# A two-layer hybrid decoder trunk on one core: the scheduler's timeline model in place of its default model

## The chip, the cores and the metric

The kernel runs on one core of one Trainium2 chip. The metric is the device time of one execution in microseconds. Three runs of the kernel before took 1592.68, 1589.84 and 1588.68 us; the median is 1589.84 us. Another execution was taken by the profiler: 1590.24 us, of which 1588.1 us lie between its first and last instruction (the span).

The engines are called as the profile calls them: PE (TensorE, matrix multiplication), PEld (its weight load), DVE (VectorE), ACT (ScalarE), POOL (GpSimd) and SP (SyncE, which issues all of this kernel's DMAs). Each engine works through a queue of its own in the order in which the program lists its instructions, and waits on semaphores for what other engines make.

## The reference

A trunk of two layers on 256 tokens of width 1024, all in float32. Each layer is a half-step SwiGLU network (inner width 2816), a token mixer, and a second half-step SwiGLU network; a last norm ends the trunk.

```python
for l in range(DEPTH):
    h = h + 0.5 * swiglu(rms_norm(h, ffn1_norm[l]), ffn1_w_in[l], ffn1_w_out[l])
    u = rms_norm(h, mix_norm[l])
    (z_s, xbc, dt_s, qkv, z_d, b_d, a_d, gate_s, gate_d) = jnp.split(u @ w_in[l], split_points, axis=-1)
    y_s = mamba2_branch(z_s, xbc, dt_s, ...)
    y_d = deltanet_branch(qkv, z_d, b_d, a_d, ...)
    merged = (jax.nn.sigmoid(gate_s) * (y_s @ ssm_w_branch[l])
              + jax.nn.sigmoid(gate_d) * (y_d @ dn_w_branch[l]))
    h = h + merged @ w_out[l]
    h = h + 0.5 * swiglu(rms_norm(h, ffn2_norm[l]), ffn2_w_in[l], ffn2_w_out[l])
return rms_norm(h, final_norm)
```

The Mamba-2 branch works on 32 heads in two chunks of 128 tokens: a short causal convolution, a decay matrix exp(a_i - a_j) for each head, and small products with it. The DeltaNet branch works on 8 heads in four chunks of 64 tokens: for each chunk a triangular matrix is inverted, and a state of 128 x 128 for each head goes from chunk to chunk.

## The kernel before

**The stream of weights.** All large weights lie in one array, cut into 504 halves of 128 x 1024 (512 KB). `load` (L95) issues the DMA of a half on SP into one of five `wraw` buffers. `prep` (L100) splits it for the products in fp32r: ACT rounds it into `whi` (L104), DVE subtracts to get the rest `wlo` (L105); there are five buffers of each. `take` (L113) hands the next half to the matmuls and traces the loads nine halves and the splits five halves ahead. A product is three matmuls: high by high, low by high and high by low (`mm3`, L210; `mm3w`, L215). The activations are split in the same way (`uTh`, `uTl`).

**The chunks.** `chan_chunk` (L238) takes two halves and runs 48 matmuls of 256 columns into one PSUM tile; `tok_chunk` (L221) and `out_chunks` (L257) run matmuls of 512 columns. Accumulators come from a pool of four PSUM tiles (`accp`), everything else that PE writes from another pool of four (`trp`). A pool `s2` of nine buffers holds the small intermediate tiles.

**The stages.** An FFN (`ffn`, L292) is 20 chunks of gate and up channels with a Silu on ACT and a product on DVE behind each, and then 22 rows of the output matrix. `close` (L275) ends each sub-layer: it adds to the residual `h` and starts the next norm (`norm_in`, L193) with raised priority, and `hold` keeps the splits of the next halves back until the norm's chain of ACT, DVE and POOL has been traced. `tc.issue_after(ins)` adds an edge that keeps instructions behind `ins` in the queue of its engine (L125, L205, L207, L334, L460, L605).

The mixer (`mixer`, L333) follows a hand-written list, `ORDER` (L38). Each word is a step: letters like `k`, `q`, `v`, `x`, `b`, `d`, `z`, `g` are chunks of weights with a convolution or an activation behind them; `K`, `Q`, `V` are the small products of a head pair; `I` the steps of the triangular inverse (`invert`, L596), `R` those of the recurrence (`recur`, L679), `D` a decay tile (`decay`, L793: a DMA of 1 MB into `dc`, two passes on DVE, an Exp on ACT, another pass on DVE), `S` and `T` the Mamba-2 products (`ssd`, L821), `N` the product with the DeltaNet output weights. The small products are in f32 and come in short bursts between the chunks.

**What sets the order.** The kernel doesn't list the queues itself. It traces its instructions, one after the other, into a tile context. When the context closes, a scheduler follows their dependencies and plays them through a model of the core's timing; whenever an engine of the model is free, it takes the ready instruction of the highest priority. The priority is the place in the trace, moved forward where `tc.high_priority` stands. The order in which the model took them becomes the order of each engine's queue, and the buffers of a pool are handed out in that order too. On the chip the queues run in that order, whatever the times really are. The context is opened in `kernel` (L1140):

```python
    with tile.TileContext(nc) as tc:
        trunk_kernel(tc, *args)
```

## Time and profile before

| | |
|---|---|
| median of three runs | 1589.84 us |
| profiled execution | 1590.24 us |
| its span | 1588.1 us |
| DVE, ACT and POOL busy | 1073.0, 879.0 and 55.1 us |
| mean granted clock of TensorE | 0.997 |
| DMA | 284.84 MB, 179 GB/s over the span |

The four FFNs take about 0 to 200, 600 to 800, 800 to 1000 and 1400 to 1588 us of the span, the two mixers about 200 to 600 and 1000 to 1400. In the answers of the trace, a row of a group gives the source line, the engine, the operation, the tiles as output<-inputs, the shapes and the count; behind the bar stand the busy time and the mean of one in ns, and behind the second bar the idle time just before them with what ended it. A row of a wait reads: engine, tile and line that waited, whom for, then the total in us, the number of times and the longest. The matmuls of PE overlap, so a row's duration is longer than the distance to the next start. The rows themselves stand in the prediction, where they are used.

### The profile page before, as it was taken

The numbers are of one execution on the slowest core, as the hardware profiler recorded it, in microseconds if no ns is written. First come the engines' busy times: TensorE is split into PE (matmuls) and PEld (weight loads), VectorE is DVE, ScalarE is ACT, GpSimd is POOL, SyncE is SP. The second block draws the span as 40 slices with busy tenths as digits, with TensorE's granted clock in tenths as the row PEclk, the third lists the DMA queues.
The fourth block names the chain that finished last, engine by engine and source line by source line (L and its number), as shares of the span: only waits on it lengthen the run. The fifth ranks groups of instructions, "written<-read, shape, count | busy, mean of one in ns | idle before, by whom it ended". The sixth has DMA issues, their size and how long they took to land.

```text
span 1588.1 us, 30449 instructions
## 1 busy us (share of the span) xinstructions
PE 1565.9 (99%) x12456; PEld 1459.8 (92%) x12456; DVE 1073.0 (68%) x1560; ACT 879.0 (55%) x1412; POOL 55.1 (3%) x60
## 2 busy tenths in 40 slices
PE   8999999999999999999999999999999999999998
PEld 7999879989999998999889987899899999989986
DVE  5555468966899766555465555698679996675554
ACT  5444468756566545444354444686655764454443
POOL 0000020000000000000000001100000000000000
PEclk9999999999999999999999999999999999999999
DMA  7555465552465446555565555655435555555552
GB/s 269 193 187 196 162 209 187 167 162 94 168 221 180 147 160 212 187 190 194 173 203 188 192 189 178 203 177 179 131 121 201 185 171 174 174 179 193 187 197 94
DMA packets 91922, 284.84 MB, mean 179 GB/s; under 512 B 22069, under 2 KB 23045, under 8 KB 90758
## 3 DMA queue, kind: packets, MB, share of 16 engines
q1 hardware_dynamic: 91782, 282.90, 53.7%
q8 instruction: 97, 1.59, 0.4%
q14 instruction: 43, 0.35, 0.1%
HBM read 280.94 MB, written 1.92 MB: 178 GB/s over the span
## 4 chain that ended last, share of the span: by engine, by line
PE 89%; DVE 5%; ACT 2%; DMA 2%; issue 1%; POOL 1%; SPq 0%; POOLq 0%; ACTq 0%; DVEq 0%
PE fc L218 9%; PE fc L217 9%; PE fc L219 9%; PE o L213 6%; PE o L211 6%; PE o L212 6%; PE b L219 3%; PE b L218 3%; PE b L217 3%; PE t L211 2%; PE t L212 2%; PE t L213 2%; PE xs L218 1%; PE xs L217 1%; PE xs L219 1%; DVE wlo L65 1%
## 5 line engine op out<-in xcount | busy, mean ns | idle before, releaser
L65 DVE TENSOR_TENSOR wlo<-wraw,whi 128x1024 fp32r<-128x1024 f32 x504 | 612.9, 1223 | 374.5 <-ACT whi L62 369.2
L62 ACT ACTIVATE whi<-wraw 128x1024 fp32r<-128x1024 f32 x504 | 529.5, 1059 | 433.7 <-PE fc L218 176.2
L217 PE MATMUL fc<-uTh,whi 128*128 128x256 f32 x1280 | 357.7, 279 | 0.0
L218 PE MATMUL fc<-uTl,whi 128*128 128x256 f32 x1280 | 357.3, 279 | 0.0
L219 PE MATMUL fc<-uTh,wlo 128*128 128x256 f32 x1280 | 357.3, 279 | 0.0
L218 PEld LDWEIGHTS fc<-uTl,whi 128*128 128x128 f32 x1280 | 240.6, 188 | 0.2
L217 PEld LDWEIGHTS fc<-uTh,whi 128*128 128x128 f32 x1280 | 240.6, 188 | 0.2
L219 PEld LDWEIGHTS fc<-uTh,wlo 128*128 128x128 f32 x1280 | 240.5, 188 | 0.0
L211 PE MATMUL o<-whi,gh 128*128 128x512 f32 x352 | 137.3, 390 | 0.0
L212 PE MATMUL o<-wlo,gh 128*128 128x512 f32 x352 | 137.2, 390 | 0.0
L213 PE MATMUL o<-whi,gl 128*128 128x512 f32 x352 | 137.0, 389 | 0.0
L217 PE MATMUL b<-bh,whi 128*128 128x256 f32 x384 | 107.8, 283 | 0.0
L218 PE MATMUL b<-bl,whi 128*128 128x256 f32 x384 | 106.8, 279 | 0.0
L219 PE MATMUL b<-bh,wlo 128*128 128x256 f32 x384 | 106.6, 279 | 0.0
L213 PEld LDWEIGHTS o<-whi,gl 128*128 128x128 f32 x352 | 66.1, 188 | 13.7
L212 PEld LDWEIGHTS o<-wlo,gh 128*128 128x128 f32 x352 | 66.1, 188 | 13.6
L211 PEld LDWEIGHTS o<-whi,gh 128*128 128x128 f32 x352 | 66.1, 188 | 13.4
L217 PE MATMUL xs<-uTh,whi 128*128 128x256 f32 x256 | 74.0, 289 | 0.0
L217 PE MATMUL g<-uTh,whi 128*128 128x256 f32 x256 | 73.0, 285 | 0.0
L218 PEld LDWEIGHTS b<-bl,whi 128*128 128x128 f32 x384 | 72.3, 188 | 0.0
L219 PEld LDWEIGHTS b<-bh,wlo 128*128 128x128 f32 x384 | 72.0, 188 | 0.0
L217 PEld LDWEIGHTS b<-bh,whi 128*128 128x128 f32 x384 | 71.8, 188 | 0.0
(264 smaller groups left out, 3224.5 us busy)
## 6 DMA issues: line engine op xcount, KB each, us to landing
wraw<-in_wst_dram SPq DMA_DIRECT2D x504, 512.0 KB, 4.2
dc<-rdram SPq DMA_DIRECT2D x8, 1024.0 KB, 8.0
nw<-in_norms_dram SPq DMA_DIRECT2D x6, 512.0 KB, 4.9
gb<-rdram SPq DMA_DIRECT2D x8, 256.0 KB, 5.6
h<-in_x_dram SPq DMA_DIRECT2D x4, 256.0 KB, 3.1
out_dram<-fo SPq DMA_DIRECT2D x4, 256.0 KB, 2.3
dq<-X SPq DMA_DIRECT2D x2, 256.0 KB, 4.5
cs<-in_cst_dram SPq DMA_DIRECT2D x1, 384.0 KB, 8.9
```

The costliest lines, as they stand in the source:

```text
L62: return A.activation(out=o, in_=i, func=func, **kw)
L65: return V.tensor_tensor(out=o, in0=a, in1=b, op=op)
L211: PE.matmul(ps, lh, rh, start=start, stop=False)
L212: PE.matmul(ps, lh, rl, start=False, stop=False)
L213: PE.matmul(ps, ll, rh, start=False, stop=stop)
L217: PE.matmul(ps, wh, mh, start=start, stop=False, skip_group_check=shared)
L218: PE.matmul(ps, wh, ml, start=False, stop=False, skip_group_check=shared)
L219: PE.matmul(ps, wl, mh, start=False, stop=stop, skip_group_check=shared)
```

## The change

The tile context is opened with one more argument. The scheduler then plays the traced instructions through another model of the core's timing, one built from lists of events (waits, engine and device holds, delays, semaphore updates), in place of the default model that gives each instruction a time on its engine. Nothing that `trunk_kernel` traces differs: the instructions, tiles, buffer counts, priorities and `issue_after` edges are the same.

```diff
-    with tile.TileContext(nc) as tc:
+    with tile.TileContext(nc, schedule_with_timeline_sim=True) as tc:
         trunk_kernel(tc, *args)
```

## The prediction

> **What bounds the kernel now.** The page comes first, for the whole span; then the table by stretches, because a mean hides stages with different limits; then what TensorE (PE) waited for.
>
> ```profile
> span 1588.1 us, 30449 instructions
> PE 1565.9 (99%) x12456; PEld 1459.8 (92%) x12456; DVE 1073.0 (68%) x1560; ACT 879.0 (55%) x1412; POOL 55.1 (3%) x60
> ```
> ```profile
> 100.00:200.00 100.00, 99.44 (x599) 88.51 (x598) 52.56 (x56) 44.83 (x53) 0.55 (x1) 1.00 0.54 181
> 300.00:400.00 100.00, 97.97 (x1020) 92.15 (x1019) 72.27 (x156) 61.58 (x145) 2.01 (x2) 0.98 0.46 143
> 400.00:500.00 100.00, 98.35 (x929) 95.99 (x928) 93.75 (x125) 65.88 (x91) 4.32 (x4) 1.00 0.56 187
> 1100.00:1200.00 100.00, 97.97 (x1082) 93.65 (x1081) 71.74 (x147) 61.42 (x135) 3.02 (x3) 1.00 0.44 141
> 1200.00:1300.00 100.00, 99.16 (x963) 96.57 (x962) 97.50 (x126) 65.86 (x89) 3.31 (x3) 1.00 0.56 193
> 1500.00:1588.00 88.00, 81.41 (x449) 70.74 (x447) 42.53 (x46) 34.27 (x44) 1.10 (x2) 0.97 0.45 150
> ```
>
> The columns after the stretch are its length, then busy microseconds of PE, weight load, DVE, ACT and POOL, then clock, DMA share and GB/s. PE is busy for 1565.9 of 1588.1 us: **22.2 us of idle PE** is the whole sum of visible gaps. 6.6 of it (88.00 - 81.41) is the end of the program, where the last norm and the stores have no matmul beside them. An FFN stretch (100 to 200) leaves 0.6 us. The mixers (about 200 to 600 and 1000 to 1400) leave 2.0 and 1.7 us in the two stretches of the first layer shown, 2.0 and 0.8 in those of the second. There DVE is nearly full as well: 93.75 and 97.50 of 100 us.
>
> ```profile
> PE hnT L186 <- DVE hn L68: 4.6, 7, 1.0
> PE xsb L835 <- ACT xsT L62: 2.5, 2, 1.6
> PE nw L157 <- DMA row<-in_norms_dram: 2.4, 1, 2.4
> PE bc L217 <- DVE ca L68: 2.0, 2, 1.0
> PE wb L627 <- ACT Y L62: 1.8, 2, 0.9
> PE f L211 <- ACT uTh L62: 0.7, 1, 0.7
> PE t L211 <- ACT uTh L62: 0.7, 1, 0.7
> ```
>
> These are all the waits of PE (total, times, longest): 14.7 us. Two kinds must be told apart. hnT, nw, f and t (8.4 us) stand at a norm or at the start, where the next matmul needs the whole residual or the first load: no other order finds work to put there, and `issue_after` and `hold` pin what surrounds them. xsb, bc and wb (6.3 us) stand inside the mixers, where PE sat at the head of its queue behind an instruction that came too early, while chunks of weights lay ready. Those 6.3 us are what a better order can take.
>
> **The change part by part.** It removes and adds no instruction of the kernel: the same matmuls, evictions and DMAs are traced, with the same tiles, buffer counts and explicit edges. What moves is the place of each in its engine's queue, and in SP's and POOL's. So the sum has three terms.
>
> *First, the early places that go.* If the other model puts the bursts of xsb, wb and the matmuls of bc where they are really ready, at best 6.3 us go; if it misjudges them as now, 0. The waits recur in both layers (twice each), so they come from a systematic misjudgement of a latency by the present order, which another model can cure or repeat. I take the middle, **-3 us**.
>
> *Second, the splits that come.* A burst of small f32 matmuls cut into a chunk costs something by itself:
>
> ```profile
> 479.93 0.28 PE L218 MATMUL b<-bl,whi 128*128 128x256 f32 x1
> 480.04 0.28 PE L219 MATMUL b<-bh,wlo 128*128 128x256 f32 x1
> 480.16 0.60 PE L890 MATMUL oT<-cs,vb 128*128 128x128 f32 x4
> 480.52 0.60 PE L217 MATMUL b<-bh,whi 128*128 128x256 f32 x3
> 480.95 0.28 PE L218 MATMUL b<-bl,whi 128*128 128x256 f32 x1
> ```
>
> Chunk matmuls start 0.11 to 0.12 us apart (479.93 to 480.04). After the burst, the three of L217, L218 and L219 that the row merges take 0.43 (480.52 to 480.95) where three steady ones take 0.35: 0.08 us, say **0.1 us a split**. From the code I count about 66 bursts in a layer (K, Q and V rests 20, scalars 5, masks 1, invert 8, recur 11, ssd 9, the turned operands of the two branches 12), 132 in all. If each were cut once more, as a model that fills every small gap might do, that is 13 us; none is 0; if it merged neighbours, up to some 3 us less. Both models fill gaps greedily, so I take a quarter more, **+3 us**.
>
> *Third, the queues of DVE, ACT and SP.* In the FFNs (about three fifths of the span) PE's own order can hardly change: one chunk follows another, each in a PSUM tile of its own, and the matmuls that accumulate into one tile depend on each other in order. What must not be late there is the split of the weights.
>
> ```profile
> L65 DVE TENSOR_TENSOR wlo<-wraw,whi 128x1024 fp32r<-128x1024 f32 x504 | 612.9, 1223 | 374.5 <-ACT whi L62 369.2
> L62 ACT ACTIVATE whi<-wraw 128x1024 fp32r<-128x1024 f32 x504 | 529.5, 1059 | 433.7 <-PE fc L218 176.2
> SPq L97 <- DVE wlo L65: 1129.0, 378, 17.4
> ```
>
> Each of the 504 halves costs 1.06 us on ACT and 1.22 on DVE. On average PE takes 1588.1 / 504 = 3.15 us for a half, so both keep up with room. ACT waits for PE to free a split buffer (176.2 us for fc alone), and SP waits 1129.0 us for DVE to free a raw buffer: the stream runs as far ahead as its five and five buffers let it. A shuffle of one or two microseconds there is hidden by these buffers: **0**. If that cover were gone, every late half would cost its lateness in full; the mixers' dense stretch is the only place where it nearly is, and that is the rival on the slow side. SP's other DMAs (8 of dc, 8 of gb, the gathers of the inverse) may change place among the loads of wraw; a block of SP that is no longer than the 17.4 us it already waits at its longest costs about nothing.
>
> The sum is -3 + 3 + 0 = 0. It is made against the profiled execution, 1590.24 us, that is the span of 1588.1 and 2.1 around it; this lies 0.4 above the median of the three runs, 1589.84. So I predict **1590 us**, with the bounds -6.3 - 3 (every avoidable wait gone, bursts merged) and +13 (every burst split) from the first two terms alone.
>
> **The rivals.**
>
> *A: faster, the better-timed order.* All three mixer waits go and a few bursts merge: 1590 - 6.3 - 2, about **1582**. For it: PE waits are the same ones in both layers. Against it: it needs nearly all of them, because anything under 4.8 us can't be told from no change, and the third term must stay at 0. More than this isn't there, since 8.4 us of waits and the end are dependencies.
>
> *B: slower, a DVE that is parked in its dense stretch.* Place: the decay tiles `dc`, at about 410 and 1200 us.
>
> ```profile
> 410.70 8.78 DMA dc<-rdram
> ```
> ```profile
> 416.76 1.23 DVE L65 TENSOR_TENSOR wlo<-wraw,whi 128x1024 fp32r<-128x1024 f32 x1 [0.17 <-ACT whi L62]
> 419.50 2.29 DVE L65 TENSOR_TENSOR dc<-dc,ac 128x2048 f32<-128x2048 f32 x1 [1.51 <-DMA dc<-rdram]
> ...
> 432.76 2.35 DVE L65 TENSOR_TENSOR wlo<-wraw,whi 128x1024 fp32r<-128x1024 f32 x2
> ```
> ```profile
> L65 DVE TENSOR_TENSOR dc<-dc,ac 128x2048 f32<-128x2048 f32 x4 | 9.1, 2285 | 1.5 <-DMA dc<-rdram 1.5
> ```
> ```profile
> 420.00:450.00 30.00, 30.00 (x295) 29.09 (x295) 29.03 (x35) 17.50 (x22) 1.92 (x1) 1.00 0.46 153
> 450.00:480.00 30.00, 28.35 (x283) 27.48 (x283) 30.00 (x47) 23.91 (x36) 1.39 (x2) 1.00 0.64 210
> ```
> ```profile
> 459.68 0.28 PE L219 MATMUL xs<-uTh,wlo 128*128 128x256 f32 x1
> 461.61 0.44 PE L835 MATMUL xsb<-cs,xsT 128*128 128x128 f32 x2 [1.65 <-ACT xsT L62]
> ```
>
> A load of dc takes 8.78 us to land; today DVE stands still only 1.5 us for it, because `wlo`, conv and recur instructions lie ahead of the subtraction in its queue. If the other model thinks the load shorter, or lets it start later, and puts the subtraction first, DVE stands still up to 8.78, that is 7.3 us more, with the wlo of the next halves behind it. From 420 to 480 it then works 59.03 of 60 us and can't make it up, and PE already runs short there (1.65 us at 461). So a parked load reaches PE almost in full: 7.3 us a layer, 14.6 in both, **about 1605**; with two of the four loads of a layer parked, 1619. It decides from the point where the extra stand exceeds DVE's spare in the stretch, 6.25 us in the first layer and 2.5 in the second (100 less 93.75 and 97.50), if none of the lead is left. For it: in this stretch two engines are full at once, so any other order is a risk and none a gain. Against it: a model that has the load shorter than it is would also have to find nothing ready to put before it.
>
> [...]
>
> *C: slower, more loads of the activation table.*
>
> ```profile
> L62 ACT ACT_TABLE_LOAD x30 | 38.5, 1283 | 16.6 <-DVE ca L68 15.4 <-PEq L1133 0.7
> ```
>
> The mixers mix Silu (conv, z), Exp (decay, masks) and Tanh (gates) on ACT; 30 loads stand there now. An order that interleaves them more finely adds 1.283 us of ACT for each. ACT has room (55% busy) except from 450 to 480, where 6.1 us are free: from the fifth added load in that stretch on (6.1 / 1.283 = 4.7), each costs PE 1.28 us. Doubling all 30 with a quarter of them uncovered gives 30 x 1.283 / 4, some 10 us: **1600**. [...]
>
> *D: the two models give the same order.* Then 1590, and the engines' sequences agree one by one. Possible for the FFNs, hardly for 800 us of mixers.
>
> **How the numbers follow.** A measurement of this kernel tells about 0.3% (4.8 us) from no change; its three runs before span 4.0 us. My forecast, little change from small gains and losses that offset, with D in it: 0.42, its own range 1585 to 1595. A: 0.20. B: 0.28. C and other misplaced bursts on PE: 0.10. So faster 0.20, the same 0.42, slower 0.38. The range goes down to 1581, just past A, because below it only the bound of 9.3 us is left, and up to 1612, between B with one load parked in each layer and B with two.
>
> **What would show it.** First term: the waits of PE for xsb, bc and wb shrink from 6.3 us. Second: more matmul groups of small shapes between chunk matmuls, with PE's busy time up by 0.1 us for each. Third: wlo and whi appear among PE's waits only if the cover is gone. B: in the waits of DVE, dc rises from 1.5 us in 420 to 520 and PE waits for wlo after it. C: the count of table loads over 30. The prediction is wrong if PE's idle time grows at the norms, where I hold the order to be pinned, if DMAs land late because SP was blocked over 17.4 us, or if the instruction counts change.

## The result and the profile after

The changed kernel is **slower by 4.2%**: 1658.54 us (median of four runs, 1654.84 to 1660.53) against 1590.67 us (four runs, 1588.68 to 1592.68); the ratio is 1.0424, 95% interval 1.0408 to 1.044. Its profiled execution took 1660.53 us with a span of 1658.7 us, 70.6 us longer than the span of before. The first two lines of its page:

```profile
span 1658.7 us, 30485 instructions
PE 1593.8 (96%) x12456; PEld 1481.0 (89%) x12456; DVE 1070.7 (65%) x1560; ACT 879.1 (53%) x1416; POOL 49.2 (3%) x60
```

The work is the same, and DVE and ACT are busy for as long as before (1070.7 and 879.1 us where it was 1073.0 and 879.0). PE is not: its idle time is 1658.7 - 1593.8 = 64.9 us instead of 22.2, which is 42.7 us more, and it is busy 27.9 us longer with the same 12456 matmuls. So there are two things to find: waits, and matmuls that last longer.

The table by stretches, with the cuts at the last `o` matmul of a sub-layer (columns as in the prediction); first two rows of the kernel before, the first mixer and the second FFN:

```profile
199.00:613.00 414.00, 409.04 (x3644) 384.32 (x3643) 326.86 (x550) 260.92 (x479) 22.85 (x22) 1.00 0.52 170
613.00:799.50 186.50, 185.83 (x1294) 172.37 (x1293) 103.70 (x114) 87.82 (x112) 2.02 (x2) 1.00 0.56 189
```

The same sub-layers of the changed kernel:

```profile
199.50:636.80 437.30, 418.95 (x3644) 392.63 (x3643) 326.99 (x550) 262.04 (x481) 21.26 (x22) 0.97 0.49 161
636.80:830.00 193.20, 188.18 (x1294) 174.12 (x1293) 103.06 (x114) 87.16 (x112) 1.11 (x2) 0.98 0.55 183
```

The mixer lost 23.3 us, the FFN 6.7. The second mixer and the two other FFNs behind a norm lost about as much each (23.8 and 7.5 to 9.0 us), and the first FFN, which has no norm between sub-layers ahead of it, 0.5. The column of the clock differs too: 0.97 and 0.98 where it was 1.00.

What PE waited for in the changed kernel (the largest rows of the view of waits):

```profile
PE f L213 <- DVE uTl L65: 13.0, 4, 4.2
PE t L213 <- DVE uTl L65: 8.4, 2, 4.2
PE b L217 <- DVE ca L68: 7.0, 2, 3.5
PE wb L627 <- ACT Y L62: 4.8, 4, 1.9
...
PE yb L627 <- DMA TT<-dq: 3.0, 2, 2.2
PE ydb L849 <- DVE xdt L65: 2.5, 2, 1.2
```

The first two rows, 21.4 us, did not exist before. They stand at the norms. DVE's timeline at the first norm between two sub-layers, in the kernel before (start, duration, what, count, and in brackets the idle time ahead of it and what ended it):

```profile
187.38 0.69 DVE L68 SCALAR_TENSOR_TENSOR h<-o,h 128x512 f32<-128x512 f32 x1 [1.08 <-PE o L213]
190.78 0.69 DVE L68 SCALAR_TENSOR_TENSOR h<-o,h 128x512 f32<-128x512 f32 x1 [2.71 <-PE o L213]
...
193.21 1.41 DVE L68 SCALAR_TENSOR_TENSOR hn<-h,zz,nw 128x512 f32<-128x512 f32 x2 [0.73 <-POOL zz L121]
194.54 1.22 DVE L65 TENSOR_TENSOR wlo<-wraw,whi 128x1024 fp32r<-128x1024 f32 x1
195.68 1.28 DVE L65 TENSOR_TENSOR uTl<-hnT,uTh 128x512 fp32r<-128x512 f32 x2
196.87 2.35 DVE L65 TENSOR_TENSOR wlo<-wraw,whi 128x1024 fp32r<-128x1024 f32 x2
```

The same place in the changed kernel:

```profile
193.44 1.29 DVE L68 SCALAR_TENSOR_TENSOR h<-o,h 128x512 f32<-128x512 f32 x2 [4.93 <-PE o L213]
...
197.43 1.42 DVE L68 SCALAR_TENSOR_TENSOR hn<-h,zz,nw 128x512 f32<-128x512 f32 x2 [0.73 <-POOL zz L121]
198.77 3.49 DVE L65 TENSOR_TENSOR wlo<-wraw,whi 128x1024 fp32r<-128x1024 f32 x3
202.17 0.68 DVE L68 SCALAR_TENSOR_TENSOR h<-o,h 128x512 f32<-128x512 f32 x1
202.78 1.21 DVE L65 TENSOR_TENSOR wlo<-wraw,whi 128x1024 fp32r<-128x1024 f32 x1
203.91 0.68 DVE L68 SCALAR_TENSOR_TENSOR h<-o,h 128x512 f32<-128x512 f32 x1
204.51 1.21 DVE L65 TENSOR_TENSOR wlo<-wraw,whi 128x1024 fp32r<-128x1024 f32 x1
205.64 1.28 DVE L65 TENSOR_TENSOR uTl<-hnT,uTh 128x512 fp32r<-128x512 f32 x2
```

Between `hn` and `uTl` stood one split of weights; now there stand five, and the residual of the other tokens. `uTl` starts 8.2 us after `hn` where it started 2.5 us after. `hn` is late as well: before, the two residual adds `h` started at 187.38 and 190.78, as PE finished one accumulator of `o` after the other; now both start at 193.44, because the order of the `o` matmuls among themselves has changed and both accumulators end late. What PE makes of it, in the kernel before:

```profile
194.02 0.66 PE L186 MATMUL hnT<-cs,hn 128*128 128x128 f32 x4 [0.56 <-DVE hn L68]
...
199.10 0.39 PE L211 MATMUL t<-whi,uTh 128*128 128x512 f32 x1
199.33 0.39 PE L212 MATMUL t<-wlo,uTh 128*128 128x512 f32 x1
```

And in the changed kernel:

```profile
199.59 1.03 PE L186 MATMUL hnT<-cs,hn 128*128 128x128 f32 x8
201.43 0.50 PE L211 MATMUL t<-whi,uTh 128*128 128x512 f32 x1 [0.81 <-ACT uTh L62]
...
206.38 0.79 PE L213 MATMUL t<-whi,uTl 128*128 128x512 f32 x1 [4.20 <-DVE uTl L65]
206.97 0.63 PE L211 MATMUL t<-whi,uTh 128*128 128x512 f32 x1
207.39 0.63 PE L212 MATMUL t<-wlo,uTh 128*128 128x512 f32 x1
```

Three things are to be seen. The transposes `hnT` stand behind all `o` matmuls (in the kernel before, at 194.02 in the midst of them, which last to 199.1), so nothing covers the chain from `hnT` over `uTh` to `uTl`: `hn` starts 2.2 us before the last `o` is through, where it started 5.9 us before. L213 stands 4.20 us for `uTl`. And the matmuls behind it start 0.42 to 0.43 us apart (206.97, 207.39, and so on to 210.38), where those of 128 x 512 start 0.23 apart otherwise (199.10 and 199.33 above): nine of them run slowed, some 1.7 us lost, with the granted clock at 0.50 from 204.2 to 211.0 us. Behind the start of the program I count ten such stretches in the trace by the distances between starts; the distances beyond the usual ones add up to 18.4 us, most of the 27.9 us that PE is busy longer. Between its start and its last norm the trace of before has one stretch of this kind, with a clock of 0.50 from 354.6 to 358.0 us; most of it falls on small products, and three matmuls of `bc` lose some 0.3 us. At the start of the program both kernels have it (the kernel before until 13.1 us, the changed one until 16.5).

### The profile page after: what moved, and what is told of

It reads as the page before. It is cut to its first block, busy times and chain, and to the rows that moved or that the text cites. A ratio compares the mean times of both kernels' runs of the same rounds, so it can differ in the third digit from the quotient of the medians.

```text
span 1658.7 us, 30485 instructions
## 1 busy us (share of the span) xinstructions
PE 1593.8 (96%) x12456; PEld 1481.0 (89%) x12456; DVE 1070.7 (65%) x1560; ACT 879.1 (53%) x1416; POOL 49.2 (3%) x60
## 4 chain that ended last, share of the span: by engine, by line
PE 76%; DVE 5%; DMA 2%; ACT 2%; issue 1%; SPq 0%; POOL 0%; POOLq 0%; DVEq 0%; ACTq 0%
PE fc L219 7%; PE fc L217 7%; PE fc L218 7%; PE o L213 4%; PE o L211 4%; PE o L212 4%; PE b L218 2%; PE b L219 2%; PE b L217 2%; PE xs L217 2%; PE xs L219 2%; PE g L217 2%; PE g L218 2%; PE xs L218 2%; PE g L219 2%; PE t L211 2%
## 5 line engine op out<-in xcount | busy, mean ns | idle before, releaser
L213 PE MATMUL o<-whi,gl 128*128 128x512 f32 x352 | 136.4, 389 | 0.0
L211 PE MATMUL o<-whi,gh 128*128 128x512 f32 x352 | 132.5, 389 | 0.0
L213 PEld LDWEIGHTS o<-whi,gl 128*128 128x128 f32 x352 | 66.1, 188 | 13.8
```

Source lines behind the costliest of these rows:

```text
L211: PE.matmul(ps, lh, rh, start=start, stop=False)
L213: PE.matmul(ps, ll, rh, start=False, stop=stop)
```

## The experiments

**How an order is put into a kernel.** Apart from `fence`, all kernels below use the default model, with the queue of every engine written out and forced by edges that make no engine wait for another. `ORDERS` holds for each engine the places of its traced instructions; the orders of both kernels were cut at places where both have the same set of instructions behind them, and each stretch between two cuts is taken from the one or the other.

```diff
+def _pin(tc, nc):
...
+        for p, q in zip(at, at[1:]):
+            tc.add_manual_dep(
+                seen[q], seen[p].name,
+                mybir.DependencyInfo(mybir.DependencyClass.NoSync, mybir.DependencyReason.DATA),
+                reason="order",
+            )
...
         trunk_kernel(tc, *args)
+        _pin(tc, nc)
```

Each kernel was timed beside the kernel before on the same chip:

| kernel | us | before | ratio (95%) |
|---|---|---|---|
| ctl_orders | 1656.86 | 1591.21 | 1.0417 (1.0401 to 1.0433) |
| joints_after | 1626.84 | 1589.54 | 1.0233 (1.0218 to 1.0249) |
| mixers_after | 1629.84 | 1589.54 | 1.0253 (1.0236 to 1.027) |
| joints_dve | 1618.80 | 1589.54 | 1.018 (1.0157 to 1.0202) |
| joints_pe | 1609.02 | 1589.54 | 1.0122 (1.0106 to 1.0139) |
| fence | 1639.95 | 1591.21 | 1.0302 (1.0286 to 1.0318) |
| bridge | 1620.03 | 1591.21 | 1.0181 (1.0164 to 1.0198) |
| mix_first | 1607.38 | 1590.37 | 1.0106 (1.0088 to 1.0124) |
| mix_mid | 1597.32 | 1590.37 | 1.004 (1.0025 to 1.0054) |
| mix_last | 1606.66 | 1590.37 | 1.0102 (1.0083 to 1.012) |
| mix_last_ca | 1607.60 | 1590.16 | 1.0109 (1.0093 to 1.0126) |
| hnT_three_later | 1589.31 | 1590.04 | 0.9997 (0.9988 to 1.0006) |
| hnT_both_later | 1590.20 | 1590.04 | 1.0002 (0.9993 to 1.0011) |

### Is it the order alone?

> The kernel before, scheduled by the default model, but with the queues of all five engines fixed to the order that the timeline model gave. If the order of the queues carries the whole change, it takes the changed kernel's time, 1658 us within 5, with the same waits at the norms (L213 on uTl, 4.2 us each). Rival: the flag does more than order the queues (other buffers, other semaphores); then it misses 1658 us by more than 8 us, to the side of the kernel before.

It took 1656.86 us, with 4.2 us as the longest wait of L213. The order of the queues carries the change; nothing else that the flag may do is needed. Why the timeline model comes to this order was not looked into.

### Norms or mixers?

`joints_after` has the changed order at the start and at the five norms between sub-layers, `mixers_after` in the interiors of the mixers (and in the first chunks behind the norms of the FFNs), each the order of before elsewhere.

> Every engine's queue is fixed: at the start of the program and at the five norms between sub-layers each engine has the order of the changed kernel, everywhere else the order of before. Theory N (the norms carry it): the changed kernel's PE stands 4.2 us at each norm for uTl and then runs some 6.8 us at half clock, about 7 to 8 us a norm, so 35 to 45 us over before, 1625 to 1635 us. Rival M (the mixers' dense stretch, as rival B of the prediction had it): the norms give under 15 us, below 1605 us.

> The other half: the order of the changed kernel inside the two mixers alone, that of before at the norms and in the FFNs. Theory N: the rest of the 70 us, 20 to 35 us over before, 1610 to 1625 us, and with the kernel with the norms alone it adds up to the changed kernel within 8 us. Rival M: over 50 us above before, 1640 us or more.

They cost 37.3 and 40.3 us. **Both matter, about equally.** `joints_after` came out as theory N had it; `mixers_after` lies 4.8 us above that theory's range and below rival M's. The sum, 77.6, is 9.7 us above the 67.9 of the whole change, where the theory allowed 8. Part of this is made by the cuts: behind the norms of the FFNs `mixers_after` has a wait that the changed kernel lacks, and its three FFNs there took 1.4 to 1.5 us more each than in the kernel before, 4.3 us together.

```profile
PE gT L322 <- DVE sg L65: 3.8, 3, 1.3
```

The rest of the difference was not followed up.

### At the norms: whose queue?

`joints_dve` takes only DVE's queue at the norms from the changed kernel, `joints_pe` only PE's:

```diff
 DVE, t=0
-hn hn wlo uTl uTl wlo wlo h h wlo zz wlo
+hn hn wlo wlo wlo h wlo h wlo uTl uTl zz
 PE, t=0 and t=1 (a cut: the order of the last o matmuls among themselves differs as well)
-o*8 hnT*4 o hnT*4 o*17 t*21 hnT*4 t hnT*4 t*2
+o*26 hnT*8 t*24 hnT*8
```

> Only DVE's queue is changed, and only at the five norms: five wlo and the two residual adds of the second token half stand ahead of uTl, where before had one wlo. Theory D (DVE's place of uTl is the cause): uTl starts about 203 instead of 195.7 us, PE waits about 4 us for it and loses 3 more to the clock, 7 us a norm, 1620 to 1630 us. Rival P (PE's order is the cause): PE still has its matmuls of the old sub-layer to cover it, under 10 us in all, below 1600 us.

> Only PE's queue is changed, and only around the five norms: the eight transposes of the normed activations stand behind all matmuls of the old sub-layer instead of among them. Theory D: PE waits 1 to 2.5 us a norm for uTh and uTl and keeps its clock, 5 to 12 us in all, 1595 to 1603 us. Rival P: most of the norms' loss, over 25 us, 1615 us or more.

DVE's queue alone costs 29.3 us, PE's alone 19.5; `joints_after`, which has both and ACT's order besides, costs 37.3. That the two sum up to more fits with each taking away cover that the other would have had. Both runs missed the range of theory D (`joints_dve` lies 1.2 us below it, `joints_pe` 6.0 above), and neither reached rival P. With DVE's queue the wait of L213 is there again, shorter, since the transposes still stand among the `o` matmuls; with PE's there is no such wait, and many small ones sum up (all waits of PE take 27.7 us, 14.7 in the kernel before). First the row of `joints_dve`, then two of `joints_pe`:

```profile
PE f L213 <- DVE uTl L65: 13.3, 6, 3.3
```
```profile
PE hnT L186 <- DVE hn L68: 7.5, 7, 1.3
PE t L211 <- ACT uTh L62: 3.5, 4, 1.6
```

A pin that keeps three of the five splits behind `uTl` was then added to the changed kernel itself, under the timeline model. It holds both halves of a split, `whi` on ACT as well as `wlo` on DVE:

```diff
@@ norm_in
                 with tc.issue_after(ins.ins):
                     ahead("prepped", n + 2, prep)
+                if add:
+                    state["fence"], state["fenced"] = done, 3
@@ ahead
-            fn(state[key])
+            if key == "prepped" and state.get("fenced", 0) > 0:
+                state["fenced"] -= 1
+                with tc.issue_after(state["fence"][0].ins), tc.issue_after(state["fence"][1].ins):
+                    fn(state[key])
+            else:
+                fn(state[key])
```

> The changed kernel, timeline model, with one pin more: at each norm the next three splits are issued behind uTh and uTl of t=0, so uTl stands ahead of all but two of the wlo instructions on DVE. Theory (DVE's queue at the norm, then the clock): L213's wait falls from 4.2 us to under 1.5 us at five norms and the half-clock stretch of 6.8 us behind it (3.4 us lost) goes or halves: 5 x 2.7 = 14 us at least, 5 x 6.5 = 32 us at most less than 1658 us, so 1626 to 1645 us. Rival (PE's place of the transposes behind the last o matmul sets the wait, whatever DVE does): PE waits as long for hnT, uTh and uTl together, and the time stays above 1650 us.

1639.95 us, 18.6 less than the changed kernel (in another batch; by the ratios 1.2%), inside the theory's range. The second FFN shows it, here as a row of the table by stretches of `fence`:

```profile
634.20:822.50 188.30, 186.59 (x1294) 172.59 (x1293) 103.13 (x114) 86.96 (x111) 1.11 (x2) 1.00 0.56 188
```

188.30 us, against 193.20 in the changed kernel and 186.50 before, at full clock: three quarters of what this norm had cost went when three of the five splits stood behind `uTl`. The two other FFNs gained as much, but the mixers hardly anything: the first one took 436.5 us (from 197.70 to 634.20), 0.8 less than in the changed kernel. The wait for `uTl` is shorter there too, but a longer one came in its place, for `uTh` of the second half of the tokens; it was 1.8 us at most in the changed kernel:

```profile
PE t L218 <- ACT uTh L62: 8.0, 4, 4.5
```

### Waiting or the clock?

`bridge` is `joints_after` with work for PE in the stall:

```diff
     def mm3(ps, lh, ll, rh, rl, start, stop):
-        PE.matmul(ps, lh, rh, start=start, stop=False)
+        extra = [PE.matmul(ps, lh, rh, start=True, stop=True).ins for _ in range(state.get("fill", 0))]
+        state["fill"] = 0
+        first = PE.matmul(ps, lh, rh, start=start, stop=False).ins
```

> joints_after (the changed order at the start and the five norms, 1626.8 us) with the first L211 matmul behind each of the five norms issued 18 times more ahead of its own (each overwrites the same bank, 18 x 0.235 = 4.2 us), so PE has work in the time in which L213 waited for uTl. No queue but PE's is touched. Theory (the clock is cut because PE stood still): the wait goes, the half-clock stretch of 6.8 us behind it goes too, 5 x 3.4 = 17 us: 1606 to 1614 us. Rival (the half clock is due to something else at the norm, or the filler only delays): 1622 us or more, with a granted clock of 0.988 as in joints_after.

The truth lies between. A row of stretches of `joints_after` and the same one of `bridge`, at the first norm:

```profile
203.00:210.00 7.00, 4.19 (x10) 3.32 (x11) 4.89 (x8) 2.29 (x5) 3.38 (x3) 0.51 0.83 272
```
```profile
203.00:210.00 7.00, 6.99 (x30) 5.32 (x29) 4.63 (x8) 2.25 (x4) 3.64 (x3) 1.00 0.82 264
```

The clock stays at 1.00 instead of 0.51, with PE's work in the stall as the one thing changed, so it was cut because PE stood still. But only 6.8 us were won, not 17. The stretch of 6.8 us at half clock begins during the wait (in the changed kernel at 204.2 us, where the wait ends at 206.38), so I had counted idle time as lost work: only 8 to 12 matmuls run slowed, 1.5 to 2.3 us a norm, 9.8 us at the five norms. And at the mixers' norms a part of the gain went into the next wait. PE's timeline of `bridge` there:

```profile
213.42 0.50 PE L214 MATMUL t<-whi,uTh 128*128 128x512 f32 x1 [1.60 <-ACT uTh L62]
```

The second wait, for `uTh` of t=1, in `joints_after`:

```profile
214.22 0.50 PE L211 MATMUL t<-whi,uTh 128*128 128x512 f32 x1 [0.30 <-ACT uTh L62]
```

It grew from 0.30 to 1.60 us: in `bridge` PE comes to this place 2.1 us earlier, but the matmul starts only 0.80 earlier (213.42 for 214.22).

### In the mixers: where?

The interiors were cut into thirds by the same method. The engines' queues depend on each other there, so one engine's order alone was not tried.

```diff
 mixers_after: all of the interior
+mix_first: t, first convs, K and V bursts, the start of the inverse
+mix_mid: bc, the inverse (yb, wb), recurrence
+mix_last: xs, xsb, ydb, yob, oT, the last convs
```

> The changed order on PE, DVE, ACT and SP only in the first third of both mixers' interiors (from the first t matmuls to the last kk and vv branches), the order of before elsewhere. Theory (each third costs by itself what the trace of mixers_after shows at its end: PE 8.3 and 1.8 us late there, with waits of uTh 2.5 and kk 1.2 to 1.8 us): +8 to +16 us, 1598 to 1606 us. Rival (the lags only defer work, and the rest of the mixer takes them back): within 4 us of the kernel before.

> The changed order on PE, DVE and ACT only in the middle third of both mixers (bc, invert, first yb and wb). Theory: +1.1 and +4.5 us of lag in mixers_after, a wait of wb on Y of 2.1 us each with some half clock: +2 to +8 us, 1592 to 1598 us. Rival (by its own it is better packed than before, since lag falls by 2 us behind it): 1584 to 1590 us.

> The changed order on PE, DVE, ACT and SP only in the last third of both mixers (ssd with xs, ydb, yob, up to the last conv). Theory (b L217 waits 4.4 us on ca, whose conv DVE takes behind ssd's work, ydb waits 1.2 us, and a half-clock stretch follows): +8 to +16 us, 1598 to 1606 us. Rival (that wait is what the first third leaves behind, since everything there runs 10 us late): within 4 us of the kernel before.

17.0, 7.0 and 16.3 us: the loss is spread, and the three add up to 40.3, as in `mixers_after`. That the sums are equal is in part chance: `mixers_after` also changes the first chunks behind the norms of the FFNs, which no third does. All three rivals fall, as no third is neutral; the first and the last third cost 1.4 and 0.7 us more than their theories had. Each has its own wait. The largest of each, in this order:

```profile
PE yb L627 <- DMA TT<-dq: 8.5, 2, 4.5
```
```profile
PE wb L627 <- ACT Y L62: 5.9, 4, 2.1
```
```profile
PE b L217 <- DVE ca L68: 7.0, 2, 3.5
```

The first is the turned inverse `TT`, which comes by DMA. The queue of SP shows that the whole chain of the inverse is late there. Its load of `X` in the kernel before and in `mix_first`:

```profile
300.85 0.34 SPq L608 DMA_DIRECT2D X<-dq  x1
```
```profile
310.44 0.34 SPq L608 DMA_DIRECT2D X<-dq  x1
```

It is issued 9.6 us later at a place where PE itself is about 3.5 us late (by the same chunk matmuls ahead of it and behind it): the new order puts off the bursts that feed the inverse. In the changed kernel PE waits less for `TT` (3.0 us); that its middle third comes to `yb` later as well would explain this, but was not looked into. That sums agree doesn't mean that the waits are the same ones.

For the last third the cause seemed plain. DVE's timeline of `mix_last`, just ahead of PE's 3.50 us wait that ends at 484.45:

```profile
481.62 2.28 DVE L65 TENSOR_TENSOR dc<-dc,ac 128x2048 f32<-128x2048 f32 x1
483.83 0.47 DVE L68 SCALAR_TENSOR_TENSOR ca<-xs,lp,ca 128x253 f32<-128x253 f32 x1
484.22 0.74 DVE L68 SCALAR_TENSOR_TENSOR og<-oT,lp,zdT 128x512 f32<-128x512 f32 x1
```

The last `ca` frees the accumulator for `b`, and a decay subtraction stands in front of it. `mix_last_ca` exchanges the two, in both mixers:

```diff
 DVE
-dc<-dc,ac, ca, og
+ca, dc<-dc,ac, og
```

> mix_last (1606.7 us) with one pair exchanged on DVE in each mixer: the last ca of the xs convolution goes ahead of the dc<-dc,ac subtraction of 2.28 us that stands in front of it; nothing else moves. Theory (DVE's order puts a decay tile ahead of the conv that frees PE's accumulator, and PE stands 3.5 us, then runs slowed): the wait falls to about 1.2 us and the half-clock stretch of 1.1 us lost goes, so 2 x 2.3 to 2 x 3.4 = 4.6 to 6.8 us less: 1600 to 1602 us. Rival (the wait is set by the whole of DVE's ssd work, or moves on to the next dc, bl or ydb): within 2 us of mix_last.

The rival holds: 1607.60 us, nothing won. The wait for `ca` shrank as the theory had it (from 7.0 to 2.6 us), but two others came, for `bh` and `og`, and the one for `bl` grew from 2.8 us:

```profile
PE b L218 <- DVE bl L65: 3.6, 4, 1.4
PE b L217 <- DVE ca L68: 2.6, 2, 1.3
...
PE b L217 <- ACT bh L62: 2.3, 2, 1.2
...
PE xsb L835 <- DVE og L68: 2.3, 2, 1.1
```

`og` stands behind `dc` as it did, and starts no earlier (484.40 for 484.22); PE now comes to `xsb` sooner and waits for it there. A few microseconds on, PE is no less late against the kernel before than in `mix_last` (6.5 us, and 6.2 there). DVE has no idle time from 475.66 to 488.7 us, so whichever instruction comes last, PE waits for it. **This fits a DVE that comes late to the whole of its work there; the place of this one instruction doesn't set the loss.** What makes DVE late is left open: it would need DVE's order without PE's.

### Can the kernel before be improved at a norm?

```diff
 PE, t=0, five norms
-o*8 hnT*4 o hnT*4 o*17
+o*11 hnT*4 o hnT*4 o*14
```

> The queues of before on all engines, with one edit: at the five norms the two hnT groups of t=0 stand three o matmuls later on PE (3 x 0.227 = 0.68 us). Theory (at a norm it is the exact place that counts: in before the trace has PE wait for hn about 0.7 us at this place, 0.88 to 0.95 us between two starts where 0.227 is usual, while uTl is ready some 2.5 us ahead of its first L213): 5 x 0.7 = 3.5 us less, 1586 to 1588 us against 1590, no new wait on uTh or uTl. Rival (the wait is only handed on, to uTh or uTl of t=0): within 1 us of before or slower.

> As hnT_three_later, and the two hnT groups of t=1 one t or f matmul later too (0.235 us, where before has 0.50 us between two starts). Theory: 5 x 0.24 = 1.2 us less than hnT_three_later, 1585 to 1587 us. Rival: t=1's first L211 has only two matmuls of slack behind the second group, so it waits for uTh and nothing is won over hnT_three_later, or it is slower.

No: 0.9997 and 1.0002. The wait of t=0 does go (PE runs on into `hnT` at 193.88, and I count 0.7 us won at each of the five norms when t=0's matmuls begin), but 0.4 to 0.9 us of it is given back some 10 us later at `hnT` of t=1, where `hn` comes from DVE at its own time. The theories' 3.5 and 4.7 us are not there; the win is handed on, as the rivals had it, the first of them at another place. None of these kernels beats the kernel before.

## Why the prediction was wrong

**The step that failed** is the sentence that puts 8.4 us of waits (hnT, nw, f, t) out of reach of the change, because "`issue_after` and `hold` pin what surrounds them". They don't. At a norm between sub-layers L207 pins two splits behind `ins`, which is `hn`, and the next three, which `take` traces, carry no pin at all; edges to `uTh` and `uTl` are made only under `if not add`, that is at the start of the program (L205). So the five splits that `hold` kept back were free to go ahead of `uTl`, and the timeline model let them; the `o` matmuls and the transposes were free as well. I had also looked only at how much could be won there. Those waits were short because the order hid a chain of some 6 us (from the residual add at 190.78 to the end of `uTl` at 196.96) behind `o` matmuls, and that cover could be lost: `joints_after` shows that it was, for 37.3 us. The prediction's own sign of being wrong, idle time of PE that grows at the norms, is what came. Another of its signs came too, but weighs nothing: the instruction count went from 30449 to 30485, and `ctl_orders` has the same 30485 by order alone.

**First term, -3 us.** Wrong in sign. The waits that I named did shrink in part: xsb is gone from the list, and bc went from 2.0 to 0.7. But wb went from 1.8 to 4.8, and the rows shown for b, yb and ydb came new with 12.5 us. I bounded the term by the waits that were there (-6.3 to 0), as if another order could only mend or repeat them. `mixers_after` lost 40.3 us, most of it in the mixers. Which place in the order makes that loss is known only by thirds and waits; the cause behind it stays open.

**Second term, +3 us.** About right in kind and of no weight: between the matmuls that read `whi` or `wlo` the traces have 115 groups of others before and 126 after, about 1 us by its own price of 0.1.

**Third term, 0.** Wrong for DVE's queue. The sentence "A shuffle of one or two microseconds there is hidden by these buffers" holds for the stream of weights, which has five and five buffers; `uTl` has only itself, the next matmuls need it at once, and it stands in the same queue. `joints_dve` prices that at 29.3 us. The working also calls the FFNs three fifths of the span; by the table by stretches they are about half, and nothing in the sum hangs on it. SP's queue is the same as before in the FFNs. In `mix_first` its load of `X` came 9.6 us later, but there the data were late, not the queue: the last `Q` came from DVE at 304.5 instead of 292.6 us.

**Rival A** fell with the first term, and **D** too: about a third of PE's instructions stand at another place.

**Rival B** had the right stretch and the wrong mechanism. No load of dc is late:

```profile
L65 DVE TENSOR_TENSOR dc<-dc,ac 128x2048 f32<-128x2048 f32 x8 | 18.3, 2285 | 4.1 <-DMA dc<-rdram 4.1
```

DVE stands 4.1 us for all eight (2.0 before), not 7.3 more for each. What held is its second half: DVE is full there, and `mix_last_ca` shows no delay made up. How a misjudged place on DVE acts is seen at the norms: in the changed kernel ACT was through with both `uTh` at 201.9 us, and `uTl` still had to wait for the five `wlo` ahead of it, from 198.77 to 205.64.

**Rival C** fell: 34 table loads instead of 30, and ACT busy 879.1 us against 879.0.

**The clock** was in no step. The prediction priced waits at their own length, but the stalls of 3.3 and 4.2 us at PE had a second price (at all five norms of the changed kernel and at four of five in `joints_dve`), since the matmuls behind it run slowed (0.42 to 0.43 us apart for 0.23). The 18.4 us counted in the changed kernel are about a quarter of its loss. A range built on misplaced bursts of 0.1 us and parked loads could not reach this.

## What to carry to other kernels

A change of the scheduler is a change of every place where the order was good by luck: ahead of it, list the serial chains between stages (here the norms), see what hides each one, and ask of each pin which instruction it names and which it leaves free. Multiply what a joint can lose, not what it has left to win, by the number of joints; where PE may come to stand, add the slowed matmuls (here 1.5 to 2.3 us a norm behind waits of 4.2 us, and some behind shorter waits with only transposes between them). And a wait that goes in the trace is won only if the next engine in the chain is ahead of its own work: filling a stall (`bridge`), moving a transpose (`hnT_three_later`) and taking a blocker away (`mix_last_ca`) gave 6.8 of 17 us, nothing and nothing.

## What the runs showed of the hardware

After a wait of 4.20 us, matmuls of 128 x 512 started 0.42 to 0.43 us apart, nearly twice the usual 0.23, at a granted clock of 0.50. With waits of 3.3 us this came at four of the five norms; rows of `joints_dve` with the clock at the second norm (0.91 over 18 us) and at the fourth (1.00):

```profile
622.00:640.00 18.00, 16.91 (x85) 14.02 (x86) 8.75 (x12) 5.99 (x8) 0.56 (x1) 0.91 0.40 135
1003.00:1024.00 21.00, 16.78 (x75) 13.04 (x74) 12.47 (x16) 12.15 (x18) 7.55 (x5) 1.00 0.60 188
```

In `joints_pe` it came at one of the five norms only (a clock of 0.92 over 21 us at the fourth, 1.00 at the others), where two waits of 1.02 and 1.65 us had nothing but eight transposes between them. The changed kernel has a place like it at the first norm: behind eight transposes at 213.68 and a wait of 1.84 us, matmuls start 0.42 to 0.43 us apart from 217.82 on. So has the kernel before: two waits of 0.90 and 0.99 us with 32 small matmuls between them, and a clock of 0.50 from 354.6 us on. No single wait has to be as long as 3.3 us for it, then, and a wait of 3.3 us isn't always followed by it. That PE's standing still is the cause was shown by `bridge`, where the clock stayed at 1.00 over the 7 us in which `joints_after` had 0.51. How long PE has to stand, and why a stall of the same length is followed by it at some norms and not at others, no run shows.
